# Turning x by transposes, the first conditioning loads from ScalarE's queue, and more of the conditioning sums on VectorE, in a hybrid convolution and attention layer

## The chip, the cores and the metric

The kernel runs on one core of a Trainium2 chip. The metric is device time in microseconds (us) for one launch. A core has TensorE (PE, matrix products into PSUM; PEld is its weight load), VectorE (DVE), ScalarE (ACT), GpSimd (POOL) and SyncE (SP). SP issues the DMA loads in the kernel before; in the profile SPq is the issuing side of SP.

## The reference

One decoder layer on x of 512 tokens by 2048 features, float32, with a conditioning vector c of 2048. What matters here is its beginning:

```python
mod = silu(c) @ w_ada + b_ada                 # 2048 -> 3 * 2048
shift, scale, gate = split(mod, 3)
h = rms_norm(x, g_pre) * (1 + scale) + shift  # rstd per token, scale and shift per feature
p = h @ w_in                                  # split into nine parts
u = cv * sigmoid(cg)                          # the first two parts of p: 2 * 1024 columns
```

Behind that come a causal depthwise convolution with a layer norm, differential attention over 8 heads, gates, two branch projections, a merge, an output projection, a norm and the residual. The change does not touch them.

## The kernel before

Products of float32 operands are written as sums of float32r parts: `split` makes a high part on ScalarE (`wh_`, `hh`) and a low part on VectorE (`wl_`, `hl`), and `mm3` (L163 is its matmul) issues three matmuls for each pair of operands. Features lie on the partitions, in 16 tiles of 128 features by 512 tokens: `xn[k]` is x times rstd, `h[k]` the normalised and conditioned input.

The opening ("start" in the code) does four things.

- *x.* SP loads x as 16 tiles, `xs[t][j]`, of 128 tokens by 512 features. `squares(t)` sums squares of a token tile, two quarters on ScalarE and two on VectorE. `scales(t0)` turns the sums of two token tiles into rstd on VectorE and puts it on a diagonal, `diag[t]`. `norm_x(j, ts)` multiplies blocks of x with that diagonal on TensorE (L236), which turns and scales them at once, into a PSUM bank `pxt`; ScalarE copies each 128x128 block into `xn` (L239).
- *Conditioning.* `ada(c0, width, npe)` makes shift and scale for `width` features. `ada_load` fetches 16 parts of `w_ada` for each (tiles `ada`, 512 KB each, seven buffers, tag `ar`). `npe` of the 16 parts go through TensorE (L273, bank `pa`): four calls with 32 columns of weights each, in four column strips of the array. The other parts are summed on VectorE (L276, L278, `acc`). In the end small products (L288, or L293 and L294, bank `pm`) bring the sums onto the partitions, VectorE adds the biases (L298 to L300), and ScalarE and VectorE make `hf` and its two parts. `GROUPS` lists the groups: first column, width, `npe`.
- *The first two parts of p.* `conv_gemm(k0, nk)` multiplies the finished features with all 2048 columns of cv and cg (bank `pc`). The first group copies its banks into `part` on ScalarE; each later group is added to `part` on VectorE (L339).
- *Order.* Up to the first group, the program order on TensorE, ScalarE and VectorE is written by hand (`manual_schedule`). Behind it `interleave` gives the order in which the convolution's steps, the next conditioning group's and what is left of x (`rest`) are emitted, and a planner arranges the engines' queues. DMA issues keep to their queue's order.

PSUM banks `g` (four) serve both `pxt` and `pc`; banks `m` (four) serve `pm`, `pa` and small things.

Of the kernel before, what the change touches and what calls it, by code (L numbers as in the profile page):

```python
# [9 lines left out]
F32 = mybir.dt.float32  # L10
# [34 lines left out]
ST = (3, 6, 6, 6, 13, 10)  # L45
# columns of shift and scale, and how many of the 16 parts of the sum TensorE takes
GROUPS = ((0, 128, 16), (128, 128, 16), (256, 256, 16), (512, 256, 16), (768, 256, 16),
          (1024, 512, 12), (1536, 512, 0))


@with_exitstack
def hybrid_trunk(ctx: ExitStack, tc: tile.TileContext, x, c, w_ada, b_ada, g_pre, g_post, w_in,
# [18 lines left out]

# [1 line left out]
    ident = cpool.tile([P, P], F32, name="ident")  # L73
# [47 lines left out]
    def rsqrt1(z, name):  # L121
        """1 / sqrt(z) for one value per partition."""
        y, t, zh = [small(1, f"{name}_{n}") for n in "yth"]
        yi, zi = y.bitcast(I32), z.bitcast(I32)
        nc.vector.tensor_single_scalar(yi, zi, 1, op=ALU.logical_shift_right)
        nc.vector.tensor_scalar(yi, yi, -1.0, 1597463007.0, op0=ALU.mult, op1=ALU.add)
        nc.vector.tensor_scalar_mul(zh, z, -0.5)
        for _ in range(3):
            nc.vector.scalar_tensor_tensor(t, y, zh, y, op0=ALU.mult, op1=ALU.mult)
            nc.vector.scalar_tensor_tensor(y, t, 1.5, y, op0=ALU.add, op1=ALU.mult)  # L130
        return y

    def paced(instruction):
        """Keep the instructions so marked in program order on their engine."""
        if PACE:
            tc.stamp_issue_order_token(instruction.ins, "paced")
        return instruction
# [35 lines left out]
    def interleave(*gens):  # L173
        """Advance generators, each given with its number of steps, in proportion."""
        gens = [[g, n, 0] for g, n in gens]
        while gens:
            g = min(gens, key=lambda e: (e[2] + 1) / e[1])
            g[2] += 1
            if next(g[0], StopIteration) is StopIteration:
                gens.remove(g)  # L180

    # ================= start: conditioning, normalised input, conv gates =================
    with tc.tile_pool(name="ps0", bufs=1, space=PSUM) as ps0, tc.tile_pool(name="ap", bufs=1) as ap:
        def gbank(name):
            return ps0.tile([P, S], F32, tag="g", bufs=4, name=name)
# [18 lines left out]
        nc.vector.memset(halves[64:, 1:2], 1.0)  # L204
        # x * rstd, features on the partitions
        xn = [page(f"xn_{kt}") for kt in range(KT)]
        ss = small(KT, "xss")

        diag = [None] * NT

        def squares(t):
            for j in range(4):
# [5 lines left out]
                else:  # L218
                    nc.scalar.activation(sq, xs[t][j], AF.Square, accum_out=ss[:, i:i + 1])

        def scales(t0):
            """diag(rstd) of 2 * 128 tokens."""
            z = small(2, f"xz_{t0}")
            nc.vector.reduce_sum(z, ss[:, 4 * t0:4 * t0 + 8].rearrange("p (t j) -> p t j", j=4),
                                 axis=mybir.AxisListType.X)
            nc.vector.tensor_scalar(z, z, 1.0 / D, EPS, op0=ALU.mult, op1=ALU.add)
            r = rsqrt(z, 2, f"xr_{t0}")
            for t in (t0, t0 + 1):
                diag[t] = ap.tile([P, P], F32, name=f"diag_{t}")
                nc.vector.tensor_scalar_mul(diag[t], ident, r[:, t - t0:t - t0 + 1])  # L230

        def norm_x(j, ts):
            for t in ts:
                pt = gbank(f"pxt_{t}_{j}")
                for i in range(4):
                    nc.tensor.matmul(pt[:, i * P:(i + 1) * P], xs[t][j][:, i * P:(i + 1) * P], diag[t],  # L236
                                     start=True, stop=True)
                for i in range(4):
                    nc.scalar.copy(xn[4 * j + i][:, t * P:(t + 1) * P], pt[:, i * P:(i + 1) * P])  # L239
                yield  # L240
# [7 lines left out]

        def ada_load(k0, nk, c0, width):
            raws = []  # L250
            for a in range(2):
                raw = ap.tile([P, nk, width], F32, tag="ar", bufs=AR, name=f"ada_{a}_{c0}_{k0}")
                nc.sync.dma_start(out=raw, in_=ada_v[:, k0:k0 + nk, a * D + c0:a * D + c0 + width])
                raws.append(raw)
            return raws

        def ada(c0, width, npe):
            """shift and scale of columns c0..c0+width, and h for these features; npe of the 16 parts of the
            sum on TensorE, the others on VectorE."""
            nk, nb, kb = 1024 // width, width // P, c0 // P  # L260
# [4 lines left out]
            for k0 in range(0, KT, nk):  # L265
                raws = ada_load(k0, nk, c0, width)
                for kk in range(k0, k0 + nk):
# [81 lines left out]
        with tc.manual_schedule(engines={mybir.EngineType.PE, mybir.EngineType.Activation, mybir.EngineType.DVE}):  # L349
            squares(0)  # L350
            squares(1)
            scales(0)
            squares(2)
            interleave((norm_x(0, (0, 1)), 1))
            squares(3)
            scales(2)
            interleave((norm_x(1, (0, 1)), 1))
            group = ada(*GROUPS[0])
            for _ in range(2):
                next(group)  # L360
            interleave((norm_x(0, (2, 3)), 1))
            next(group)
            early[0, 0, 0] = conv_wsplit(0, 1, 0, 4, 0, C_CV)
            interleave((group, 1))
        for g, a, c0 in ((0, 1, C_CG), (1, 0, C_CV)):
            early[0, g, a] = conv_wsplit(0, 1, g, 4, a, c0)
        rest = [norm_x(j, ts) for j, ts in ((1, (2, 3)), (2, range(4)), (3, range(4)))]
        rest = (None for g in rest for _ in g)
        for i, (c0, width, _) in enumerate(GROUPS[:-1]):
# [25 lines left out]

    # ================= main part =================
    ps1 = ctx.enter_context(tc.tile_pool(name="ps1", bufs=1, space=PSUM))
# [16 lines left out]
    def gemm2(src, c0, rhs, nk, name):  # L414
        """Two output tiles [128 features, tokens] of columns c0..c0+256."""
        ps = [bank("g", 4, f"pg_{name}_{f}") for f in range(2)]
# [10 lines left out]

    # lambda
    lt = small(HD, "lt")
# [10 lines left out]

# [1 line left out]
    cvo = [None] * 8  # L442
# [40 lines left out]

# [1 line left out]
    vt = [None] * 2  # L485
# [72 lines left out]
    for pair in range(4):  # L558
# [13 lines left out]
        for f in range(2):  # L572
            head(pair * 2 + f, qs[f], ks[f])
# [1 line left out]
    # h = [[B11, B12], [B21, B22]], halves of the features by halves of the tokens:  # L575
    # T1 = B11 - B12, T2 = B22 + T1, T3 = B12 - B22, T4 = B21 - T2
    H2 = S // 2
# [55 lines left out]

    # ================= gates =================
    front.close()
# [13 lines left out]
    def gemm_blocks(src, c0, name):  # L649
        """Two output tiles [128 features, tokens] of h @ src[:, c0:c0+256], by 7 products of 2x2 blocks.  # L650

        a11 a12 / a21 a22: features by halves of the sum.  Returns (c11 in PSUM, [.. c12], [c21 c22])."""
        r1 = wraw(src, 0, KH, c0, 256, f"{name}_1")
# [7 lines left out]
        def prod(ps, w, b, first):  # L661
            """Add a product to what the bank holds (read between the products)."""
            hi, lo = w
            for k in range(KH):
                mm3(ps[:, :H2], (hi[:, k, :], lo[:, k, :]), b[k], first and k == 0, k == KH - 1, not first, ordered)
            pump(rate[0])
# [31 lines left out]
    def silu2(i, z, ta, tb):  # L698
        """2 * silu of the two output tiles."""
        g0, g1 = temp(f"g0_{i}"), temp(f"g1_{i}")  # L700
# [7 lines left out]

    # channel layer norm and swish of the convolution, its gate
    hg = small(8, "hg")  # L710
# [84 lines left out]

    # ================= branch projections, gated merge =================
    # 2 * (sigmoid(m_conv) * y_conv + sigmoid(m_attn) * y_attn)
    def gemm_y(src, c0, rhs, name):
# [42 lines left out]
    def gate(n):  # L841
        """Columns n * 512.. of (c @ w_ada's gate part + b_ada) * g_post, on all partitions."""
        bg = temp(f"bg_{n}")
# [45 lines left out]

    # ================= output projection, tokens on the partitions =================  # L890
    fss = small(16, "fss")
# [15 lines left out]
    for n in range(4):  # L907
# [19 lines left out]
        if n < 3:  # L927
            for t in range(NT):
                out_evac(n, t, ps[t])
    # what the first three parts give to the mean square  # L930
    nc.vector.reduce_sum(zp, fss.rearrange("p (t n) -> p t n", n=4)[:, :, :3], axis=mybir.AxisListType.X)
# [46 lines left out]
```

## Time and profile before

| what | value |
|---|---|
| time, median of 3 runs | 1445.52 us (1444.5 to 1447.1) |
| span of the profiled execution | 1448.4 us |
| TensorE busy | 1413.6 us, 98% |
| VectorE busy | 1053.0 us, 73% |
| ScalarE busy | 534.2 us, 37% |
| first convolution matmul (`pc`) starts | 33.05 us |
| first matmul of the attention's values (`pv`) starts | about 258 us |

The profile is of one execution; its span lies 2.9 us above the median of the runs, and the page shows no time of the execution outside its span. Busy time counts instructions at work; a busy TensorE is not TensorE at its peak, since matmuls are pipelined. The granted clock (PEclk) is given as a share of 2.4 GHz; 0.50 is 1.2 GHz.

### The profile page before, as it was taken

To read this page: it belongs to the slowest core of one execution; us is meant where nothing else is said; L and a number is where in the kernel's file an instruction comes from. 1 tells how busy PE (TensorE), PEld (TensorE's weight loads), DVE (VectorE), ACT (ScalarE), POOL (GpSimd) and SP (SyncE) were. 2 spreads that over 40 slices of the span, in tenths; PEclk is the share of its full clock that TensorE was granted. 3 is DMA by queue.
4 is the path that set the end of the run, shared out by engine and by line. 5 is a ranking of instruction groups with operands and counts; after the bars stand their busy time and mean duration, and the time that the engine had idled before them with its cause. 6 is when DMAs were issued, how large, how long until landed. Compare 5 with 4: busy or idle time off the path is not lost.

```text
span 1448.4 us, 20732 instructions
## 1 busy us (share of the span) xinstructions
PE 1413.6 (98%) x8191; PEld 1200.4 (83%) x8191; DVE 1053.0 (73%) x1720; ACT 534.2 (37%) x901; POOL 1.8 (0%) x8
## 2 busy tenths in 40 slices
PE   4999999999999999999999999999999999999997
PEld 4776778787777877688999999999998888888885
DVE  4466785988888888588997888877767448656645
ACT  4622233223444244434544444444445323222230
POOL 0000000000000000000000000000000000000000
PEclk9999999999999999999999999999999999999999
DMA  9878653232223323124654555533369647267543
GB/s 285 264 255 291 215 167 130 88 131 87 66 81 102 102 67 109 66 95 135 209 165 160 187 178 191 188 121 132 126 226 349 224 137 233 95 207 243 189 145 145
DMA packets 178466, 238.62 MB, mean 165 GB/s; under 512 B 7793, under 2 KB 118722, under 8 KB 177474
## 3 DMA queue, kind: packets, MB, share of 16 engines
q1 hardware_dynamic: 178370, 237.31, 49.5%
q8 instruction: 64, 1.05, 0.3%
q14 instruction: 32, 0.26, 0.1%
HBM read 210.02 MB, written 27.26 MB: 164 GB/s over the span
## 4 chain that ended last, share of the span: by engine, by line
PE 93%; DVE 3%; DMA 1%; ACT 1%; issue 1%; SPq 0%; DVEq 0%; ACTq 0%
PE pc L163 12%; PE pw L163 12%; PE py_ya L163 6%; PE py_yc L163 6%; PE pv L163 6%; PE pg_k L163 6%; PE pg_q L163 5%; PE pg_az L163 5%; PE x_ma L163 5%; PE x_mc L163 5%; PE y_mc L163 3%; PE z_mc L163 3%; PE z_ma L163 3%; PE y_ma L163 3%; PE x_cz L163 2%; PE y_cz L163 2%
## 5 line engine op out<-in xcount | busy, mean ns | idle before, releaser
L468 DVE SCALAR_TENSOR_TENSOR cacc<-u,cw,cacc 128x511 f32<-128x511 f32 (+14 forms) x240 | 164.4, 729 | 0.0
L163 PE MATMUL pc<-hh,wh_c 128*128 128x512 f32 x256 | 102.9, 408 | 1.1 <-ACT hh L141 1.1
L163 PE MATMUL pc<-hh,wl_c 128*128 128x512 f32 x256 | 101.0, 398 | 1.5 <-DVE wl_c L142 1.4
L163 PE MATMUL pc<-hl,wh_c 128*128 128x512 f32 x256 | 101.7, 397 | 0.0
L339 DVE TENSOR_TENSOR part<-pc,part 128x512 f32<-128x512 f32 x96 | 66.0, 691 | 46.9 <-PE pc L163 45.8
L163 PE MATMUL pw<-wh_o,mh 128*128 128x512 f32 x224 | 89.0, 397 | 0.0
L163 PE MATMUL pw<-wh_o,ml 128*128 128x512 f32 x224 | 87.3, 390 | 0.0
L163 PE MATMUL pw<-wl_o,mh 128*128 128x512 f32 x224 | 87.2, 389 | 0.0
L141 ACT CAST wh_c<-wr_c 128x1024 fp32r<-128x1024 f32 (+1 forms) x36 | 34.6, 960 | 112.5 <-PE pc L163 85.6
L141 ACT CAST wh_o<-wr_o 128x1024 fp32r<-128x1024 f32 x28 | 29.5, 1053 | 104.5 <-PE pw L163 93.0
L163 PEld LDWEIGHTS pc<-hh,wh_c 128*128 128x128 f32 x256 | 49.0, 192 | 17.9 <-issue 3.3
L856 DVE SCALAR_TENSOR_TENSOR accg<-adag,cact,accg 128x512 f32<-128x512 f32 x60 | 45.0, 750 | 24.0 <-DMA adag<-in_w_ada_dram 22.8
L163 PEld LDWEIGHTS pc<-hh,wl_c 128*128 128x128 f32 x256 | 49.1, 192 | 15.7 <-issue 2.5
L142 DVE TENSOR_TENSOR wl_o<-wr_o,wh_o 128x1024 fp32r<-128x1024 f32 x28 | 34.2, 1221 | 34.0 <-ACT wh_o L141 34.0
L163 PEld LDWEIGHTS pc<-hl,wh_c 128*128 128x128 f32 x256 | 49.3, 192 | 10.2 <-issue 0.4
L163 PE MATMUL pv<-wh_v,hh 128*128 128x512 f32 x128 | 51.2, 400 | 0.9 <-DVE part L339 0.9
L142 DVE TENSOR_TENSOR wl_c<-wr_c,wh_c 128x1024 fp32r<-128x1024 f32 (+1 forms) x36 | 39.7, 1104 | 16.5 <-ACT wh_c L141 16.4
L163 PE MATMUL pg_q<-hh,wh_q 128*128 128x512 f32 x128 | 51.1, 399 | 0.0
L163 PE MATMUL pg_k<-hh,wl_k 128*128 128x512 f32 x128 | 51.1, 399 | 0.0
L163 PE MATMUL pg_q<-hl,wh_q 128*128 128x512 f32 x128 | 50.9, 397 | 0.0
L163 PE MATMUL pg_az<-hl,wh_az 128*128 128x512 f32 x128 | 50.7, 396 | 0.0
L163 PE MATMUL pv<-wl_v,hh 128*128 128x512 f32 x128 | 50.6, 395 | 0.0
(358 smaller groups left out, 4312.7 us busy)
## 6 DMA issues: line engine op xcount, KB each, us to landing
ada<-in_w_ada_dram SPq DMA_DIRECT2D x64, 512.0 KB, 6.1
wr_ma<-in_w_in_dram SPq DMA_DIRECT2D x16, 1024.0 KB, 5.5
wr_mc<-in_w_in_dram SPq DMA_DIRECT2D x16, 1024.0 KB, 5.0
adag<-in_w_ada_dram SPq DMA_DIRECT2D x32, 512.0 KB, 4.2
wr_o<-in_w_o_dram SPq DMA_DIRECT2D x16, 1024.0 KB, 5.1
wr_c<-in_w_in_dram SPq DMA_DIRECT2D x28, 512.0 KB, 5.0
wr_v<-in_w_in_dram SPq DMA_DIRECT2D x8, 1024.0 KB, 5.2
wr_q<-in_w_in_dram SPq DMA_DIRECT2D x8, 1024.0 KB, 5.3
```

Of the source, the lines that this page charges most:

```text
L141: nc.scalar.copy(hi, src)
L142: i = nc.vector.tensor_tensor(lo, src, hi.bitcast(F32), op=ALU.subtract)
L163: mm = nc.tensor.matmul(ps, a[p], b[q], start=start and i == 0, stop=stop and i == 2, skip_group_check=more)
L339: nc.vector.tensor_tensor(part[i], ps[f], part[i], op=ALU.add)
L468: paced(nc.vector.scalar_tensor_tensor(cvo[t][:, s:], u[t][:, :S - s], wj, cvo[t][:, s:], op0=ALU.mult, op1=ALU.add))
L856: nc.vector.scalar_tensor_tensor(acc, raw[:, k, :], s1, acc, op0=ALU.mult, op1=ALU.add)
```

## The change

`GROUPS` gives fewer parts to TensorE in four of the seven groups. x is turned with transposes that don't need rstd, into one bank per feature tile with all four token tiles; rstd is spread over the partitions by a product of ones and the diagonal (bank `prs`), copied to `rsb` by ScalarE, and VectorE multiplies each `pxt` bank with it into `xn`. Of the 16 feature tiles eight are turned inside the hand-written order and eight behind it. The four loads of the first conditioning group are issued on ScalarE's queue, ahead of the hand-written part.

```diff
-GROUPS = ((0, 128, 16), (128, 128, 16), (256, 256, 16), (512, 256, 16), (768, 256, 16),
-          (1024, 512, 12), (1536, 512, 0))
+GROUPS = ((0, 128, 16), (128, 128, 16), (256, 256, 12), (512, 256, 10), (768, 256, 10),
+          (1024, 512, 8), (1536, 512, 0))
...
+        rsb = ap.tile([P, S], F32, name="rsb")
+        prs = mbank("prs0")
         def scales(t0):
...
             for t in (t0, t0 + 1):
-                diag[t] = ap.tile([P, P], F32, name=f"diag_{t}")
-                nc.vector.tensor_scalar_mul(diag[t], ident, r[:, t - t0:t - t0 + 1])
-        def norm_x(j, ts):
-            for t in ts:
-                pt = gbank(f"pxt_{t}_{j}")
-                for i in range(4):
-                    nc.tensor.matmul(pt[:, i * P:(i + 1) * P], xs[t][j][:, i * P:(i + 1) * P], diag[t],
-                                     start=True, stop=True)
-                for i in range(4):
-                    nc.scalar.copy(xn[4 * j + i][:, t * P:(t + 1) * P], pt[:, i * P:(i + 1) * P])
+                diag = ap.tile([P, P], F32, tag="diag", bufs=2, name=f"diag_{t}")
+                nc.vector.tensor_scalar_mul(diag, ident, r[:, t - t0:t - t0 + 1])
+                nc.tensor.matmul(prs[:, t * P:(t + 1) * P], ones, diag, start=True, stop=True)
+            ts = slice(t0 * P, (t0 + 2) * P)
+            nc.scalar.copy(rsb[:, ts], prs[:, ts])
+        pxt = [None] * KT
+        def turn(ks, ts):
+            for k in ks:
+                if pxt[k] is None:
+                    pxt[k] = gbank(f"pxt_{k}")
+                for t in ts:
+                    nc.tensor.transpose(pxt[k][:, t * P:(t + 1) * P],
+                                        xs[t][k // 4][:, k % 4 * P:(k % 4 + 1) * P], ident)
+        def norm_x(ks):
+            for k in ks:
+                nc.vector.tensor_tensor(xn[k], pxt[k], rsb, op=ALU.mult)
+        def turn_norm(ks):
+            for k in ks:
+                turn((k,), range(NT))
+                norm_x((k,))
                 yield
...
-        def ada_load(k0, nk, c0, width):
+        def ada_load(k0, nk, c0, width, queue=nc.sync):
...
-                nc.sync.dma_start(out=raw, in_=ada_v[:, k0:k0 + nk, a * D + c0:a * D + c0 + width])
+                queue.dma_start(out=raw, in_=ada_v[:, k0:k0 + nk, a * D + c0:a * D + c0 + width])
...
+        begun = {(0, k0): ada_load(k0, 8, 0, 128, nc.scalar) for k0 in (0, 8)}
...
-                raws = ada_load(k0, nk, c0, width)
+                raws = begun.pop((c0, k0), None) or ada_load(k0, nk, c0, width)
...
         with tc.manual_schedule(engines={mybir.EngineType.PE, mybir.EngineType.Activation, mybir.EngineType.DVE}):
-            squares(0)
-            squares(1)
-            scales(0)
-            squares(2)
-            interleave((norm_x(0, (0, 1)), 1))
-            squares(3)
-            scales(2)
-            interleave((norm_x(1, (0, 1)), 1))
+            for t in range(NT):
+                squares(t)
+                turn(range(4), (t,))
+                if t % 2:
+                    scales(t - 1)
+            norm_x(range(4))
             group = ada(*GROUPS[0])
+            next(group)
+            turn(range(4, 8), range(NT))
+            norm_x(range(4, 8))
             for _ in range(2):
                 next(group)
-            interleave((norm_x(0, (2, 3)), 1))
-            next(group)
             early[0, 0, 0] = conv_wsplit(0, 1, 0, 4, 0, C_CV)
             interleave((group, 1))
...
-        rest = [norm_x(j, ts) for j, ts in ((1, (2, 3)), (2, range(4)), (3, range(4)))]
-        rest = (None for g in rest for _ in g)
+        rest = turn_norm(range(8, KT))
```

## Rows read from the trace of the kernel before

**Rows 1.** The page's busy times, with shares of the span and instructions

```profile
PE 1413.6 (98%) x8191; PEld 1200.4 (83%) x8191; DVE 1053.0 (73%) x1720; ACT 534.2 (37%) x901; POOL 1.8 (0%) x8
```

**Rows 2.** Windows by stage: stretch, length, busy PE, PEld, DVE, ACT, POOL, clock, DMA

```profile
33.05:56.20 23.15, 23.15 (x162) 20.14 (x162) 6.21 (x16) 18.73 (x60) 0.00 (x0) 0.93 0.78 249
56.20:72.20 16.00, 16.00 (x118) 11.00 (x117) 12.84 (x23) 4.48 (x11) 0.00 (x0) 1.00 0.88 294
72.20:99.90 27.70, 27.65 (x167) 20.05 (x166) 19.75 (x30) 8.87 (x12) 0.00 (x0) 1.00 0.83 279
...
126.80:153.80 27.00, 27.00 (x139) 15.90 (x138) 15.78 (x23) 3.00 (x3) 0.00 (x0) 0.98 0.93 321
153.80:207.50 53.70, 52.16 (x225) 42.42 (x225) 46.39 (x68) 14.89 (x17) 0.00 (x0) 0.95 0.59 190
```

**Rows 3.** The chain that ended last, to 34 us: start, duration, what

```profile
13.92 3.25 SPq L253
...
17.21 8.02 DMA ada<-in_w_ada_dram
...
33.05 1.07 PE pc L163 x2
```

**Rows 4.** DMA of the first 60 us, in 40 slices of 1.5 us

```profile
GB/s 0 87 238 317 149 173 388 396 393 389 362 307 290 291 291 318 371 311 290 292 296 271 348 279 320 370 362 368 352 349 369 139 22 210 175 35 58 295 40 264
```

**Rows 5.** Timeline of SP's issues: start, duration, what, count

```profile
12.55 6.38 SPq L253 DMA_DIRECT2D ada<-in_w_ada_dram  x4
```

**Rows 6.** Timelines of VectorE and TensorE ahead of the first convolution matmul

```profile
17.58 0.68 DVE L216 CUSTOM_DVE_ANT_0 xsq<-x 128x512 f32<-128x512 f32 x1
...
21.53 0.16 DVE L224 TENSOR_REDUCE xz<-xss 128x2 f32<-128x8 f32 x1 [3.26 <-ACT xsq L219]
...
24.10 0.48 DVE L230 TENSOR_SCALAR diag<-ident,xr_y 128x128 f32<-128x128 f32 x2
...
29.73 0.34 PE L288 MATMUL pm<-halves,accp 128*128 128x2 f32 x2
```

**Rows 7.** Bursts on TensorE, from the chain that ended last, to 250 us

```profile
51.82 4.46 PE pxt L236 x40
...
64.23 1.86 PE pa L273 x32
...
69.04 0.34 PE pm L288 x4
...
136.91 0.97 PE pa L273 x2
...
205.94 1.68 PE pm L294 x16
```

**Rows 8.** TensorE by line and form, to 260 us: busy, mean ns, idle before

```profile
L273 PE MATMUL pa<-ada,c 128*32 128x256 f32 x192 | 12.8, 384 | 0.0
L273 PE MATMUL pa<-ada,c 128*32 128x512 f32 x48 | 9.1, 601 | 0.0
```

**Rows 9.** Timeline of TensorE in the attention stage, around a burst of transposes

```profile
611.92 0.60 PE L533 MATMUL pt<-ident,t 128*128 128x128 f32 x4
612.27 0.48 PE L163 MATMUL pg_az<-hh,wl_az 128*128 128x512 f32 x1
```

**Rows 10.** VectorE by line and form, to 260 us

```profile
L339 DVE TENSOR_TENSOR part<-pc,part 128x512 f32<-128x512 f32 x96 | 66.0, 691 | 46.9 <-PE pc L163 45.8
...
L278 DVE SCALAR_TENSOR_TENSOR acc<-ada,cact,acc 128x512 f32<-128x512 f32 x36 | 25.3, 747 | 0.0
...
L284 DVE COPY accp<-pa 128x256 f32<-128x256 f32 x3 | 1.3, 419 | 0.0
```

**Rows 11.** Windows of TensorE: stretch, length, busy time, granted clock, DMA

```profile
149.77:153.76 3.99, 3.99 (x33) 0.87 1.06 386
153.76:159.56 5.80, 5.80 (x15) 0.50 0.40 138
205.78:207.48 1.70, 1.70 (x17) 1.00 0.96 326
```

More of the change, by code (lines that the diff above doesn't have):

```diff
@@ L207, in hybrid_trunk @@
         ss = small(KT, "xss")
-        diag = [None] * NT
         def squares(t):
```

## The prediction

> **What bounds the kernel now.** I read the busy shares first: TensorE is busy for 98% of the span, so what counts is work taken from it, work added to it, and time in which it is made to wait [rows 1]. Then the stages of the opening in one table of windows [rows 2]. Before 33.05 us, when the first convolution matmul starts [rows 3], TensorE still waits; from there it is busy for all but 0.05 us of the stages shown up to 153.8 us, while VectorE has room in each: 16.9 us of 23.2, 3.2 of 16.0, 8.0 of 27.7 and 11.2 of 27.0. Only in 153.8 to 207.5 us is VectorE nearly full (46.4 of 53.7), and there TensorE is idle for 1.5 us. The reader should keep two budgets apart: the instant at which the convolution starts, and TensorE's work after it. The profiled span is 1448.4 us, 2.9 us above the median of the three runs, 1445.5; the page gives no time outside the span, so I work out differences and take them off the median. A change of 0.2%, 2.9 us, is about what a measurement of this kernel can tell from none.
>
> **Turning x.** Before, a 128x128 product with a diagonal is two matmul records, and 40 of these records took 4.46 us, 111 ns each [rows 7], so 223 ns a block. Of the 64 blocks, 24 are done ahead of 33.05 us and 40 after it: 8.9 us. After the change 32 of the 64 are turned ahead of the convolution and 32 behind. A true transpose is one record in the attention stage, and a burst of four held TensorE for 0.35 us, from 611.92 to 612.27 us [rows 9]: 88 ns each, 2.8 us for 32. Saved: 6.1 us (at 56 ns each, half of a product's record, 7.1; with 0.09 us more a burst for the change of kind that I cannot see in the row, 5.4). The Trainium skill, "TensorE: Matmul & The Clock Gate", Terms, calls its transpose mode four times faster for FP32; the row gives 2.5 times, and by the rule 7.1 us would be saved. I go by the row.
>
> **The multiplication by rstd** moves from 64 ScalarE copies to 16 VectorE products of 128x512 out of PSUM, priced like the part additions, 0.69 us [rows 10]. Eight of them lie in 33 to 56 us, where VectorE has 16.9 us free, so 5.5 us cost nothing there; without that cover they would be 5.5 us. The other eight lie on the chain into the first matmul (below).
>
> **Conditioning sums.** TensorE loses 4, 6 and 6 of 16 parts in the three groups of 256 columns and 4 of the remaining 12 in that of 512. Today they are 192 records with 12.8 us and 48 records with 9.1 us busy [rows 8]. Four calls run side by side: 32 records of 256 columns took 1.86 us, 58 ns each, but two records of 512 columns alone still held TensorE for 0.97 us [rows 7]. So half-filled rounds cost as much as full ones, and dropping parts saves less than in proportion. For 256 columns 128 records remain: 7.4 us if packed, 12 if each step is a burst by itself; I take 9.9, 2.9 us saved. For 512 columns 32 records remain, one part in each of eight steps: 3.7 us packed, 7.8 as eight rounds of 0.97; I take 7.1, 2.0 us saved. Together 4.9 us (2.1 to 10.8).
>
> **The final sums get dearer.** A group done wholly on TensorE closes with one small product for each block: four records, 0.34 us. As soon as VectorE holds a share, each block needs four products, as in the last group: sixteen records for 16 columns' worth, 1.68 us [rows 7]. A 256-column group then needs sixteen too, so three groups cost 3 x 1.34 = 4.0 us more (5.0 at the 125 ns a record that the 512-column group shows in its 3.99 us for 32 [rows 11]).
>
> TensorE's work after its start: -6.1 - 4.9 + 4.0 = -7.0 us (-2.5 to -13.9).
>
> **VectorE's new work.** 32 multiply-adds of 128x256 at some 0.42 us (the copy of that shape; the 512 form is 0.75) are 13.4 us, and 8 of 128x512 are 6.0 [rows 10]. By stage: 3.4 us into 3.2 spare, 5.0 into 8.0, 5.0 into the stage that follows, for which I assume the same room, 6.0 into 11.2. It is late in the first alone, but a part addition that stands behind a sum keeps one of four PSUM banks from the next convolution matmul. I charge 1.3 us (0 if the planner always puts sums into the gaps; 9 if nearly half of the 19 us falls on TensorE).
>
> **The instant at which the convolution starts.** Today the last square ends at 18.3 us, but the scales wait until 21.53 because ScalarE copies turned blocks before its own last squares [rows 6]; the conditioning landed only at 25.23 [rows 3]. After the change both go. If x lands as now: scales and diagonals 3.05 us (21.53 to 24.58) after 18.4, giving 21.5; two small products and a 256-column copy, 1.1; eight products on VectorE in a row, 5.5, giving 28.1; behind them in VectorE's program order the copy of the conditioning sum, 0.3; then small product to first matmul as today, 29.73 to 33.05, less one weight cast that can go earlier, 2.7: 31.1 us, 2.0 earlier. So a new serial stretch eats most of the removed waits.
>
> But x will not land as now. The conditioning's 2.1 MB start beside x's 4.2 MB on the same DMA engines, which moved 290 to 396 GB/s from 9 to 24 us and less in the slices from 3 to 9 us (877 against some 1560 over four slices of 1.5 us: about 1.0 MB of room) [rows 4]. The 2.1 MB took 7 us at 290 GB/s; less what fits into the room, x is 0 to 4.5 us later. I take 3: start at 34.1 us, 1.0 later than now (bounds -2.0 and, with ScalarE held up, +4.3, below). Issuing from ScalarE frees 6.38 us of SP's issuing [rows 5], and SP's weight loads follow x sooner; they were not what the first matmul waited for.
>
> **Sum:** -7.0 + 1.3 + 1.0 = -4.7 us, 1440.8 us.
>
> **Rivals.**
> *The opening is late (0.20).* On SP the third conditioning load held the queue for 3.25 us, and the four took 6.38 us where an issue without a hold-up takes about 0.4; as I read it, they stood behind packets still waiting [rows 3, 5]. On ScalarE the same hold-up stands in front of its tanh and of eight squares, and VectorE's squares and scales, some 11 us in a row, stand behind that tanh. If the fourth issue ends near 14 us instead of 3, the convolution starts at 35.5 to 37.4 us, up to 4.3 later than now, and the time is -7.0 + 1.3 + 4.3: 1444.1 us. Against it: alone on the engines, the first half of these 2.1 MB would be gone within 4 us [rows 4]. The Trainium skill says in "Trainium Kernel Development and Optimization", Key Constraints, that issuing from several engines only saves issue time, since all queues share 16 DMA engines and interleave; by that rule x is always late and this rival or its milder form holds. The trace has one data queue, so no row here shows two interleaving.
>
> *VectorE becomes the bound (0.14), the one on the other side.* The place is the three stages from 56 to 127 us: a sum ahead of a part addition holds a PSUM bank. For it: the 153.8 to 207.5 us stage, where sums fill VectorE and TensorE idles 1.5 us and its matmuls spread. Against: from 72 us the spare time is above what is added. Without stalls the change is -6.0 us, so with 6 us on TensorE it is a wash and from 8.9 us, nearly half of the 19, it is slower by over 0.2%. At 9 us: 1448.5 us.
>
> *The clock falls in the new final sums (0.06).* After 3.99 us of single-column products the granted clock was 0.50, 1.2 GHz, from 153.76 to 159.56 us: 5.80 us for the work of 2.9 [rows 11]. Three new such stretches would cost 8.7 us: 1449.5. Against: these are 1.7 us each, and the stretch of that length at 205.78 us was at full clock. One dip leaves 1443.7, so it decides from the third.
>
> *More gain (0.10).* Sums near their packed price (-8 instead of -4.9) and x landing as now: -6.1 - 8 + 4.0 - 2.0 = -12.1 without stalls, 1433.4 us.
>
> **How the numbers follow.** The forecast itself has 0.50, with a range of its own from 1437 to 1444. Shares of faster by over 0.2%, within 0.2%, and slower: forecast 0.42, 0.08, 0; late opening 0.04, 0.09, 0.07 (with stalls too); VectorE 0.01, 0.05, 0.08; clock 0, 0.01, 0.05; more gain 0.10, 0, 0. Sums 0.57, 0.23, 0.20. The range for 8 in 10 runs from 1434 to 1449: it leaves out the most of "more gain" and the far half of VectorE and clock.
>
> **What the profile after would show.** Half as many records for turning x, in bursts of four near 0.35 us; about 64 fewer conditioning records of 256 columns but bursts that stay near 1 us; sixteen small records at three group ends, 1.7 us each; the first convolution matmul between 31 and 36 us, behind eight VectorE products; VectorE over 0.9 busy from 56 to 72 us with TensorE idle below 1 us; TensorE's stretch from first convolution matmul to 258 us today shorter by 4 to 8 us. Wrong would be: ScalarE's squares starting after 14 us, TensorE idle on a part addition or an accumulator, or a granted clock of 0.5 after a new final sum.

## The result, and the profile after

The change makes the kernel slower: 1455.81 us (median of four runs, 1454.79 to 1457.22) against 1445.78 (four runs, 1444.5 to 1447.1); the ratio is 1.0062 [1.0043, 1.0082], some 6 to 12 us. The forecast was 1440.8, with a range from 1434 to 1449.

| point in the profiled execution, us | before | after |
|---|---|---|
| VectorE's last square of x ends | 18.26 | 24.84 |
| first convolution matmul starts | 33.05 | 41.19 |
| first matmul of the attention's values starts | 258.29 | 263.06 |
| span | 1448.4 | 1453.0 |

From the attention's first matmul on, the traces of both take 1190 us, and so does the trace of every kernel below: what the traces differ by is decided in the opening. The page's busy times of after answer to [rows 1]; TensorE has 5.5 us less to do, and the kernel is longer all the same:

```profile
span 1453.0 us, 20544 instructions
...
PE 1408.1 (97%) x8091; PEld 1194.9 (82%) x8091; DVE 1077.4 (74%) x1776; ACT 523.0 (36%) x839; POOL 1.8 (0%) x8
```

The timeline of after, up to the first convolution matmul (start, duration, what; in brackets the idle time before it and what ended it):

```profile
0.73 9.05 ACTq L268 DMA_DIRECT2D ada<-in_w_ada_dram  x4
...
6.57 11.60 SPq L95 DMA_DIRECT2D x<-in_x_dram  x12
9.81 1.28 ACT L195 ACT_TABLE_LOAD   x1 [9.81 <-DMA x<-in_x_dram]
...
24.15 0.69 DVE L214 CUSTOM_DVE_ANT_0 xsq<-x 128x512 f32<-128x512 f32 x1 [0.64 <-DMA x<-in_x_dram]
...
25.66 0.16 DVE L225 TENSOR_REDUCE xz<-xss 128x2 f32<-128x8 f32 x1 [0.81 <-ACT xsq L217]
...
32.19 0.23 DVE L447 TENSOR_TENSOR lt<-lamv 128x64 f32<-128x64 f32 x1 [3.16 <-DMA lamv<-in_lam_k_dram]
...
32.59 4.29 DVE L249 TENSOR_TENSOR xn<-pxt,rsb 128x512 f32<-128x512 f32 x7
...
41.19 1.20 PE L163 MATMUL pc<-hh,wh_c 128*128 128x512 f32 x4 [1.02 <-ACT hh L141]
```

Three things are to be seen. ScalarE issues until 9.8 us, and its table load waits for that. The last squares wait for x's DMA: the one that began at 17.58 before [rows 6] begins at 24.15. And VectorE, done with the scales, stands idle for 3.16 us ahead of a product `lt` that belongs to the attention's lambda and has nothing to do with x: the planner put it ahead of the eight products with rstd, and its operand had not landed.

What each queue moved between 1 and 11 us (packets, MB, share of 16 engines), in after:

```profile
q10 hardware_dynamic: 2691, 1.36, 48.1%
q1 hardware_dynamic: 715, 1.16, 42.5%
```

and in before, where SP's queue is alone:

```profile
q1 hardware_dynamic: 1309, 2.23, 75.0%
```

q10 is ScalarE's queue with the conditioning, q1 is SP's with x. Together they moved 0.3 MB more than SP's queue alone, so almost everything that the conditioning got, x lost: 1.07 MB by 11 us. By 15 us even the 0.3 MB are gone, since from 9 to 15 us before moved 392 GB/s and after 332. From 1 to 15 us after shows

```profile
q10 hardware_dynamic: 4154, 2.10, 55.3%
q1 hardware_dynamic: 1025, 1.71, 42.1%
```

and before

```profile
q1 hardware_dynamic: 2168, 3.80, 83.5%
```

The two queues moved 3.81 MB, the one 3.80: x had lost the conditioning's whole 2.1 MB.

The bursts of x's transposes behind the start, from the chain that ended last in after:

```profile
45.21 0.59 PE pxt L244 x4
...
48.57 0.87 PE pxt L244 x8
...
52.47 0.87 PE pxt L244 x8
...
56.62 1.46 PE pxt L244 x12
```

They answer to these `pxt` bursts of before and to the one of 4.46 us in [rows 7]:

```profile
38.68 1.09 PE pxt L236 x8
...
42.52 0.89 PE pxt L236 x8
...
43.53 1.00 PE pxt L236 x8
...
47.30 1.78 PE pxt L236 x16
```

3.79 us for 32 transposes, against 9.22 for the 80 records of before: 5.4 us saved. TensorE's conditioning records and small products in after, by line and form (answers to [rows 8]), up to 263 us:

```profile
L290 PE MATMUL pa<-ada,c 128*32 128x256 f32 x128 | 11.6, 386 | 0.0
L311 PE MATMUL pm<-ones,acc 128*128 128x1 f32 x56 | 9.1, 248 | 0.0
L290 PE MATMUL pa<-ada,c 128*32 128x512 f32 x32 | 8.7, 603 | 0.0
L310 PE MATMUL pm<-halves,accp 128*128 128x1 f32 x40 | 6.9, 241 | 0.0
```

A third of the records went, and 1.2 us of 12.8 and 0.4 of 9.1 with them. The chain shows why: a burst is priced by rounds, of which a part costs as much as the whole. 10 records of 256 columns took as long as 12, and a pair of 512 columns nearly 1 us by itself:

```profile
62.01 0.99 PE pa L290 x12
...
72.06 0.98 PE pa L290 x10
...
143.96 0.98 PE pa L290 x2
```

In before 16 records of 256 columns took no longer than these 10:

```profile
56.29 1.00 PE pa L273 x16
```

The two waits of TensorE between 154 and 207 us that cost more than 1 us, in after:

```profile
182.84 0.50 PE L163 MATMUL pc<-hh,wl_c 128*128 128x512 f32 x1 [2.75 <-DVE wl_c L142]
195.78 0.50 PE L163 MATMUL pc<-hh,wl_c 128*128 128x512 f32 x1 [1.73 <-DVE wl_c L142]
```

Before has one, of 1.43 us (at 191.05). On VectorE four sums stand ahead of the first of these weight parts, in program order:

```profile
178.92 2.73 DVE L295 SCALAR_TENSOR_TENSOR acc<-ada,cact,acc 128x512 f32<-128x512 f32 x4
181.56 1.22 DVE L142 TENSOR_TENSOR wl_c<-wr_c,wh_c 128x1024 fp32r<-128x1024 f32 x1
```

The two traces differ by 4.6 us and the timed runs by 10.0. A span lies 1.7 to 2.2 us below the time of the same execution in every one for which both are known (after: 1453.0 and 1454.79 us). So the traced execution of before, with its span of 1448.4, stands for some 1450 us, 4 to 5 above its median, and that of after is 1.0 below its own, which makes up the other 5.4 us. The granted clock tells why in part. Between its start and 258 us the profiled execution of before was at 0.50 for 10.2 us, 6.8 of them in the stretch that [rows 11] shows and 3.41 here (stretch, length, busy TensorE, clock, DMA):

```profile
33.26:36.67 3.41, 3.41 (x9) 0.50 0.97 315
```

Up to 263 us after has only 160.50 to 163.91, behind the group of 1024:

```profile
156.70:160.10 3.40, 3.40 (x34) 1.00 0.90 307
160.50:163.91 3.41, 3.41 (x10) 0.50 0.00 0
```

So before spent 6.8 us more than after at half the clock, which is 3.4 us of work. Such stretches vary between executions (the mean granted clock of before's timed runs goes from 0.993 to 0.998), so differences of 1 to 3 us between two traces are not read as effects below; the ratios of timed runs decide.

### The profile page after: what moved, and what is told of

Same layout as the page of the kernel before. It is cut to its first block, busy times and chain, and to the rows that moved or that the text cites. A ratio compares the mean times of both kernels' runs of the same rounds, so it can differ in the third digit from the quotient of the medians.

```text
span 1453.0 us, 20544 instructions
## 1 busy us (share of the span) xinstructions
PE 1408.1 (97%) x8091; PEld 1194.9 (82%) x8091; DVE 1077.4 (74%) x1776; ACT 523.0 (36%) x839; POOL 1.8 (0%) x8
## 4 chain that ended last, share of the span: by engine, by line
PE 93%; DVE 3%; DMA 2%; ACT 1%; issue 1%; SPq 0%; DVEq 0%; ACTq 0%
PE pc L163 12%; PE pw L163 12%; PE pg_k L163 6%; PE py_ya L163 6%; PE py_yc L163 6%; PE pv L163 6%; PE pg_az L163 5%; PE pg_q L163 5%; PE x_ma L163 5%; PE x_mc L163 5%; PE y_mc L163 3%; PE z_mc L163 3%; PE z_ma L163 3%; PE y_ma L163 3%; PE x_cz L163 2%; PE y_cz L163 2%
## 5 line engine op out<-in xcount | busy, mean ns | idle before, releaser
L163 PE MATMUL pg_q<-hh,wl_q 128*128 128x512 f32 x128 | 50.5, 395 | 0.0
```

The source lines that it names most:

```text
L163: mm = nc.tensor.matmul(ps, a[p], b[q], start=start and i == 0, stop=stop and i == 2, skip_group_check=more)
```

## The experiments

The change has three parts: the loads on ScalarE's queue (L), the new `GROUPS` (G) and the turning (T). Five runs undo or isolate one part or two, and with before and after they make a table of all combinations but one (G with L). Before was timed again beside each set of runs, with medians from 1447.02 to 1448.14 us, so ratios are compared here and not times.

| kernel | parts | ratio to before | first convolution matmul, us |
|---|---|---|---|
| before | none | 1 | 33.05 |
| e3 | L | 1.0049 [1.0037, 1.0062] | 38.08 |
| e6 | G | 1.0024 [1.0015, 1.0034] | 32.22 |
| e5 | T | 0.9995 [0.9985, 1.0005] | 32.60 |
| e1 | T, G | 1.0032 [1.0021, 1.0044] | 31.40 |
| e2 | T, L | 1.0020 [1.0011, 1.0029] | 40.66 |
| after | T, G, L | 1.0062 [1.0043, 1.0082] | 41.19 |

**e1, the conditioning loads back on SP.** The theory: the late start is due to the loads beside x. The rival: VectorE's serial stretch makes it.

```diff
-        begun = {(0, k0): ada_load(k0, 8, 0, 128, nc.scalar) for k0 in (0, 8)}
+        begun = {}
```

> The changed kernel, with the first four conditioning loads back on SP's queue behind x. Theory A (the loads on ScalarE's queue are what costs: they share the DMA engines with x and hold ScalarE until 9.8 us): the last square on VectorE is back from 24.2 to near 17.6 us, the first convolution matmul comes at 33 to 36 us instead of 41.2, and the time falls from 1455.8 to 1448 to 1451 us. Theory B (the conditioning sums on VectorE cost it, not the opening): the first matmul may move, but the time stays above 1453 us. Theory C (the eight products with rstd in a row are the late part): the first matmul stays at 39 us or later.

Measured: 1452.5 us, ratio 1.0032. The start is at 31.40 us and the last square ends at 17.58: the loads cause the late start, 9.8 us of it. But the time fell by only 0.3%, some 4 us, to a value between those expected by its theories A and B. One reason is a new wait, of TensorE on the weights' fourth tile. Its row in TensorE's timeline of e1:

```profile
41.48 0.50 PE L163 MATMUL pc<-hh,wh_c 128*128 128x512 f32 x1 [3.37 <-DVE xn L249]
```

VectorE's next product into `xn`, which frees a PSUM bank for TensorE, stood in program order behind a weight part whose cast had waited for its DMA. The rest shows only in the clock: the profiled execution, 1448.9 us at a mean granted clock of 0.996, was the fastest of six; the other five took 1452.2 to 1452.8 at 0.992 or 0.993. In which stretch they lost it, no trace here shows.

**e2, the old groups.** The theory: the new sums cost time. The rival: they save, and the opening alone costs.

```diff
-GROUPS = ((0, 128, 16), (128, 128, 16), (256, 256, 12), (512, 256, 10), (768, 256, 10),
-          (1024, 512, 8), (1536, 512, 0))
+GROUPS = ((0, 128, 16), (128, 128, 16), (256, 256, 16), (512, 256, 16), (768, 256, 16),
+          (1024, 512, 12), (1536, 512, 0))
```

> The changed kernel with the conditioning sums divided between the engines as before the change. Theory A: the sums are nearly even, 4 to 5 us less on TensorE against 4 us more in the final small products, so the time stays within 3 us of 1455.8. Theory B: the time falls by 6 us or more, to under 1450 us.

Measured: 1450.5 us, ratio 1.0020. With the start as late as after's, 217.2 us instead of 221.9 lie between it and the attention's first matmul. The new groups cost 4.7 us there; the waits behind `wl_c` shrink to the one of 1.43 us that before has. So the theory holds, and the late opening costs the rest.

**e3, before with the loads on ScalarE alone.**

```diff
-        def ada_load(k0, nk, c0, width):
+        def ada_load(k0, nk, c0, width, queue=nc.sync):
...
-                nc.sync.dma_start(out=raw, in_=ada_v[:, k0:k0 + nk, a * D + c0:a * D + c0 + width])
+                queue.dma_start(out=raw, in_=ada_v[:, k0:k0 + nk, a * D + c0:a * D + c0 + width])
...
+        begun = {(0, k0): ada_load(k0, 8, 0, 128, nc.scalar) for k0 in (0, 8)}
...
-                raws = ada_load(k0, nk, c0, width)
+                raws = begun.pop((c0, k0), None) or ada_load(k0, nk, c0, width)
```

> The kernel before with one edit: the first four conditioning loads issued from ScalarE's queue. Theory A: ScalarE is held for some 9 us and x lands some 6 us later, so the first convolution matmul comes 3 to 7 us after the 33.05 us of before and the time rises by 3 to 7 us, to 1449 to 1453 us. Theories B and C: within 2 us of 1445.8, since the conditioning lands earlier than the 25.2 us that the first matmul waited for.

Measured: 1454.9 us, ratio 1.0049, the dearest single part. The last square ends at 24.33 us and the convolution starts 5.0 us late. Lambda's wait is here too, though nothing of VectorE's work was edited: SP issues lambda's first load at 27.95 us here, at 49.98 in before, and the planner put its product into the opening.

**e4, lambda's products behind the opening.** After, with the products of `lt` held behind the last `u`.

```diff
+        last_u = [None]
...
-                        nc.vector.scalar_tensor_tensor(u[i], th, 1.0, part[i], op0=ALU.add, op1=ALU.mult)
+                        last_u[0] = nc.vector.scalar_tensor_tensor(u[i], th, 1.0, part[i], op0=ALU.add, op1=ALU.mult)
...
-    for i in range(2):
-        nc.vector.tensor_tensor(lt, lamv[:, 2 * i, :], lamv[:, 2 * i + 1, :], op=ALU.mult)
-        nc.vector.reduce_sum(le[:, i:i + 1], lt, axis=mybir.AxisListType.X)
+    with tc.issue_after(last_u[0].ins):
+        for i in range(2):
+            nc.vector.tensor_tensor(lt, lamv[:, 2 * i, :], lamv[:, 2 * i + 1, :], op=ALU.mult)
+            nc.vector.reduce_sum(le[:, i:i + 1], lt, axis=mybir.AxisListType.X)
```

> The changed kernel with VectorE's lambda products put behind its last instruction of the convolution input, where the changed kernel has the first of them between the diagonals and the eight products with rstd, waiting 3.2 us for a load of lambda's rows. Theory A with this wait as a part of the loss: the first convolution matmul comes 1.5 to 2.5 us earlier than 41.2 and the time falls by as much, to 1453 to 1454.5 us. Rival: the eight products wait for ScalarE's copy of rstd and for turned banks anyway, and the time stays within 0.7 us of 1455.8.

Measured: 1454.1 us, ratio 1.0044 [1.0031, 1.0056]; its interval and after's overlap. In its timeline the eight products begin at 30.55 us, right behind `rsb`:

```profile
30.55 4.92 DVE L249 TENSOR_TENSOR xn<-pxt,rsb 128x512 f32<-128x512 f32 x8 [1.33 <-ACT rsb L234]
```

The convolution starts at 38.11 us, so lambda's place cost 3.1 of the 9.8 us between e1 and after, and the loads the other 6.7. Of the 3.1, 2.0 are the later begin of the eight products. The other 1.0 goes with the 16 transposes among them, which took 2.35 us in e4, 3.68 in after, and 3.67 in e8 below at a granted clock of 0.50. Of the 3.1, 2.2 came back at 47.05 us as a wait of TensorE behind the fourth weight tile, cast at 45.05, as in e1: a start that is earlier than its weights gains little.

**e5, the turning alone.** After with both edits of e1 and e2.

```diff
+GROUPS = ((0, 128, 16), (128, 128, 16), (256, 256, 16), (512, 256, 16), (768, 256, 16),
+          (1024, 512, 12), (1536, 512, 0))
...
+        begun = {}
```

> The changed kernel with both the loads on SP's queue and the old division of the sums: of the change, only x turned by transposes and multiplied by rstd on VectorE is left. If the two other parts are what costs, each by itself: the first convolution matmul at 31 to 33 us, TensorE's stretch from there to the attention's values 217 to 220 us (217.2 with the old sums, 225 to 226 with the new ones), and a time 4 to 8 us under the kernel before beside it. If the transposes' serial stretch on VectorE costs: no faster than the kernel before.

Measured: 1447.06 us against 1448.14, ratio 0.9995: no difference. 32 transposes behind the start are cheap here too, but the timelines of ScalarE and TensorE in e5 have these rows:

```profile
40.52 0.62 ACT L141 CAST wh_c<-wr_c 128x512 fp32r<-128x512 f32 x1 [4.17 <-DMA wr_c<-in_w_in_dram]
...
42.52 0.50 PE L163 MATMUL pc<-hh,wh_c 128*128 128x512 f32 x1 [3.25 <-DVE xn L249]
```

Before has no such wait up to 60 us: the cast of that tile runs at 38.19 us there, and bursts of turning x stand between the first steps. 3.25 us, of the 5.4 that the transposes save, are handed to the weights. Not all of it is TensorE being earlier: the tile is later too. SP's queue has seven conditioning loads between the third weight tile and the fourth where that of before has five, so the fourth goes out later. In e5

```profile
33.56 1.27 SPq L151 DMA_DIRECT2D wr_c<-in_w_in_dram  x2
```

and in before

```profile
32.02 0.34 SPq L151 DMA_DIRECT2D wr_c<-in_w_in_dram  x1
```

**e6, the new groups alone**, in before.

```diff
+GROUPS = ((0, 128, 16), (128, 128, 16), (256, 256, 12), (512, 256, 10), (768, 256, 10),
+          (1024, 512, 8), (1536, 512, 0))
```

> The kernel before with only the new division of the sums. Theory B as now seen (final small products +4 us, 1 to 3 us saved on the sums, VectorE in the way for 3 to 6 us): the stretch from the first convolution matmul to the attention's values grows from 225 to 229 to 233 us and the time by 4 to 8 us. Rival, as predicted: within 2 us of the kernel before.

Measured: 1451.7 us, ratio 1.0024, 3.5 us and a little less than the 4 to 8 expected: the sums cost without any other part. The waits in TensorE's timeline of e6 are after's:

```profile
178.23 0.50 PE L163 MATMUL pc<-hh,wl_c 128*128 128x512 f32 x1 [2.75 <-DVE wl_c L142]
191.18 0.50 PE L163 MATMUL pc<-hh,wl_c 128*128 128x512 f32 x1 [1.73 <-DVE wl_c L142]
```

From the table the part G costs 0.24% (before to e6), 0.37% (e5 to e1) and 0.42% (e2 to after). The part L costs 0.49% (before to e3), 0.25% (e5 to e2) and 0.30% (e1 to after). The part T makes no clear difference without L (-0.05% from before to e5, +0.08% from e6 to e1), but saves 0.29% with it (e3 to e2): there the convolution starts at 38 us or later, and no wait for the fourth weight tile follows in either trace.

**e7 and e8, sharing or ScalarE held?** After's loads sit on a second queue and also hold ScalarE's instructions for 9 us. e7 leaves two of the four loads there, e8 issues all four from GpSimd.

```diff
-        begun = {(0, k0): ada_load(k0, 8, 0, 128, nc.scalar) for k0 in (0, 8)}
+        begun = {(0, 0): ada_load(0, 8, 0, 128, nc.scalar)}
```

> The changed kernel with only the first two of the four loads on ScalarE's queue, which SP's issues of before let through without a hold-up. If ScalarE held up is the larger part: ScalarE's tanh runs by 5 us, VectorE starts its squares as before, and the first convolution matmul comes at 34 to 36 us, 5 or more earlier than 41.2. If sharing the DMA engines with x is: half the bytes, so x is some 3 us late instead of 6.5, and the first matmul comes at 37 to 39 us.

```diff
-        begun = {(0, k0): ada_load(k0, 8, 0, 128, nc.scalar) for k0 in (0, 8)}
+        begun = {(0, k0): ada_load(k0, 8, 0, 128, nc.gpsimd) for k0 in (0, 8)}
```

> The changed kernel with the four first loads issued from GpSimd's queue instead of ScalarE's: they still start beside x, but ScalarE is not held. If sharing the DMA engines is the cause: the last square still ends at 22 to 25 us and the first convolution matmul comes at 37 us or later. If the hold-up of ScalarE is: the first convolution matmul comes at 32 to 35 us. A slow start of the loads from GpSimd would show as a conditioning sum that comes after the eight products.

Measured: e7 1454.7 us, ratio 1.0048 [1.0033, 1.0063], last square 22.62, start 36.32 us, between the two ranges expected. e8 1455.85 us, ratio 1.0057 [1.0042, 1.0071]. The timeline of e8:

```profile
0.74 1.28 ACT L195 ACT_TABLE_LOAD   x1 [0.74 <-PEq L979]
1.73 1.01 POOL L268 DMA_DIRECT2D ada<-in_w_ada_dram  x1
...
3.31 2.65 POOL L268 DMA_DIRECT2D ada<-in_w_ada_dram  x3
...
25.75 0.16 DVE L225 TENSOR_REDUCE xz<-xss 128x2 f32<-128x8 f32 x1 [1.53 <-ACT xsq L217]
...
41.27 0.96 PE L163 MATMUL pc<-hh,wh_c 128*128 128x512 f32 x3 [1.02 <-ACT hh L141]
```

ScalarE is free from the beginning, its squares wait for x instead, and the convolution starts at 41.27 us, where after's starts at 41.19. Both stand behind lambda's wait (2.61 us in e8), which could hide a difference ahead of it; but the second scales, ahead of that wait, begin at 25.75 us against 25.66 in after. That ScalarE was held cost nothing; the bytes beside x made it late. Half of the bytes (e7) leave x's last square 4.4 us late instead of 6.6. The convolution of e7 starts 4.9 us earlier than after's, more than these 2.2, since lambda's first product stands behind the eight products there and waits 1.31 us; in the ratios the intervals of e7 and after overlap.

**e9, the opposite of G.** Before with all 16 parts of the group of 1024 on TensorE.

```diff
-          (1024, 512, 12), (1536, 512, 0))
+          (1024, 512, 16), (1536, 512, 0))
```

> The kernel before with one number changed the other way: in the group at column 1024 TensorE takes all 16 parts instead of 12. If half-filled rounds and dearer final products are why giving parts to VectorE does not pay: the sums of 512 columns stay at 8 to 9 us for a third more parts, the final products of that group fall from 4.0 to 0.7 us, VectorE loses 6 us of work, the drop of the clock behind the products is gone, and the time falls by 4 to 8 us. Rival, by work in proportion: 2 us more on the sums against 3.3 us less, within 2 us of the kernel before.

Measured: 1439.53 us against 1447.02, ratio 0.9943 [0.9931, 0.9955]. By line and form, up to 262 us:

```profile
L273 PE MATMUL pa<-ada,c 128*32 128x512 f32 x64 | 8.0, 598 | 0.0
...
L288 PE MATMUL pm<-halves,accp 128*128 128x2 f32 x24 | 3.0, 230 | 0.0
L294 PE MATMUL pm<-ones,acc 128*128 128x1 f32 x16 | 1.8, 245 | 0.0
```

64 records take less than the 48 of before (9.1 us [rows 8]), as every round is filled. The group closes with 8 small products in 0.79 us where [rows 11] shows 33 records in 3.99, the wait of 1.43 us behind `wl_c` is gone, and behind the products TensorE's clock stays up, as the window of the next 20 us shows (columns as above):

```profile
145.95:165.95 20.00, 20.00 (x89) 1.00 0.89 298
```

As an estimate from the two traces, 1.1 us on the records, 3.2 on the closing, 1.4 of wait and 3.4 of clock (6.8 us at half in before) add to some 9 us, where the ratio gives 8.2. The fall of the clock goes with that closing: the traces of all twelve kernels with 32 small products there show 0.50 for 3.4 or 6.8 us, beginning in the closing or within 1.5 us behind it, and those of e9 and e11, with 8, show none. For this group the move that the change makes has the wrong sign; for the groups of 256 columns e9 says nothing.

**e10, only tiles 8 to 15 turned**, with the opening of before up to the start.

```diff
+        rsb = page("rsb")
+
+        def turn_norm(ks):
+            prs = mbank("prs0")
+            for t in range(NT):
+                nc.tensor.matmul(prs[:, t * P:(t + 1) * P], ones, diag[t], start=True, stop=True)
+            nc.scalar.copy(rsb, prs)
+            for k in ks:
...
+                    nc.tensor.transpose(pt[:, t * P:(t + 1) * P],
+                                        xs[t][k // 4][:, k % 4 * P:(k % 4 + 1) * P], ident)
+                nc.vector.tensor_tensor(xn[k], pt, rsb, op=ALU.mult)
+                yield
...
-        rest = [norm_x(j, ts) for j, ts in ((1, (2, 3)), (2, range(4)), (3, range(4)))]
+        rest = [norm_x(1, (2, 3)), turn_norm(range(8, KT))]
```

> The kernel before with its own opening, where only the eight feature tiles behind the hand-written part are turned by transposes and multiplied by rstd on VectorE. If the transposes' saving of some 5.5 us is real and was only eaten by an earlier wait for the fourth weight tile: the first convolution matmul stays at 33 us, that wait is 1 us or less, and the time falls by 3 to 5 us. If the wait comes back in full: within 1.5 us of the kernel before.

Measured: 1444.09 us, ratio 0.9974 [0.9963, 0.9985]. The start is at 33.64 us, and no wait on weights follows up to 60 us. The first tiles are still turned by products there, and SP issues the fourth weight tile behind five conditioning loads, as in before, at 32.61 us; the run doesn't part the two. Here the transposes show their gain.

**e11, e9 and e10 together.**

```diff
-          (1024, 512, 12), (1536, 512, 0))
+          (1024, 512, 16), (1536, 512, 0))
...
+        rest = [norm_x(1, (2, 3)), turn_norm(range(8, KT))]
```

> The two edits together (the eight later tiles turned, all 16 parts on TensorE in the group at column 1024). If they act in different stages the gains add, 7 to 12 us under the kernel before; if both only fill a wait that is set elsewhere, no more than the larger of the two alone.

Measured: 1436.74 us against 1447.02, ratio 0.9922 [0.9909, 0.9934]: faster than both kernels, and nearly the sum of the two (0.83%).

**e12, e5 with the fourth weight tile loaded ahead** of the 256-column conditioning loads on SP.

```diff
+        held = [None]
...
-                queue.dma_start(out=raw, in_=ada_v[:, k0:k0 + nk, a * D + c0:a * D + c0 + width])
+                with tc.issue_after(held[0].ins) if held[0] else nullcontext():
+                    queue.dma_start(out=raw, in_=ada_v[:, k0:k0 + nk, a * D + c0:a * D + c0 + width])
...
+                fourth = wp.tile([P, 1, 4 * P], F32, tag="wr", name="wr_c_0_1_1")
+                held[0] = nc.sync.dma_start(out=fourth, in_=w_in[0].rearrange("(t p) n -> p t n", p=P)[
+                    :, 0:1, C_CG + 4 * P:C_CG + 8 * P])
+                early_raw[0, 1, 1] = fourth
```

> The turned x alone (loads on SP, old sums), with the convolution's fourth weight tile issued ahead of the 256-column conditioning loads instead of behind three of them. If the 3.2 us that TensorE stood at 42.5 us in the run without this edit was a wait for that tile (it landed at 40.4 us): it lands at 35 to 37.5 us, the wait is under 1 us, and the time is 2 to 3 us below that run, some 3 us under the kernel before. If the wait is VectorE's or ScalarE's own order: it stays above 2 us and the time stays that of the kernel before.

Measured: 1446.34 us against 1447.46, ratio 0.9991 [0.9982, 1.0]; e5 had 0.9995. The wait became shorter, not absent (TensorE's timeline of e12):

```profile
40.75 0.50 PE L163 MATMUL pc<-hh,wh_c 128*128 128x512 f32 x1 [2.09 <-DVE xn L249]
```

SP had moved the lambda loads ahead of the tile, which was issued at 34.93 us only. So this run doesn't show what the whole turning gives with the tile in time; e10 shows it for half the tiles, and e3 to e2 with a late start.

## Why the prediction was wrong, point by point

Its sum, term by term, with what the traces of before and after show (us):

| term | predicted | measured |
|---|---|---|
| turning x behind the start | -6.1 | -5.4 (9.22 to 3.79) |
| conditioning sums off TensorE | -4.9 | -1.6 (12.8 + 9.1 to 11.6 + 8.7) |
| final small products | +4.0 | +4.0 (three stretches like 70.38 to 72.06 us, for 0.34 each) |
| waits for VectorE | +1.3 | +3.0 (2.75 + 1.73 less 1.43) |
| the instant at which the convolution starts | +1.0 | +8.1 (33.05 to 41.19) |
| sum | -4.7 | +8.1 |

+8.1 lies inside the +6 to +12 of the timed runs. The execution of before that was profiled lost 3.4 us more to the clock than that of after; less these, it is 4.7, and the spans differ by 4.6. Of the 12.8 us by which the sum is off, 7.1 are the start, 3.3 the conditioning sums, 1.7 the waits and 0.7 the turning.

**The instant at which the convolution starts failed, by 7.1 us.** The case "if x lands as now" was right: 31.1 us forecast, 31.40 in e1. The step that failed is "x is 0 to 4.5 us later. I take 3", and in it the room of about 1.0 MB that the conditioning was to fill in the slices from 3 to 9 us. By 11 us the two queues had moved only 0.3 MB more than one, and by 15 us no more at all: x was behind by the conditioning's whole 2.1 MB. Its last square came 6.6 us later, which is 2.1 MB at some 320 GB/s. A gap in the throughput row was taken for room. With e4, 6.7 us of start, against e1, are due to this sharing. The other 3.1 are lambda's place, which the prediction did not have: SP's loads were followed past the weights only, not to the loads that moved up, and the planner placed their consumer ahead of the products. The rival "the opening is late" had the right place and the wrong cause. Its hold-up is there (ScalarE's issuing ends at 9.8 us), but e8 shows that it costs nothing. The rule cited with it, of the Trainium skill, "Trainium Kernel Development and Optimization", Key Constraints, that issuing from several engines saves only issue time because all share the 16 engines, agrees with these runs: with another issuer x was as late (second scales at 25.75 against 25.66 us, convolution at 41.27 against 41.19). None of the three signs of being wrong that the prediction names stands behind the loss; the start at 41.19 us, where it expected 31 to 36, does.

**The conditioning sums were mis-sized, by 3.3 us.** "Half-filled rounds cost as much as full ones" was right, but the values taken, between packed and rounds, lay too far from rounds: the 1.6 us saved are less than the lowest bound given (2.1), and the 32 records of 512 columns took 8.7 us, more than the 7.8 of eight rounds. With the final small products, rightly sized at +4.0, the move costs where it was forecast to save 0.9: 128 records for 192 save 1.2 us and the closings cost 4.0. e6 and e2 show that the move as a whole costs, and e9 that the opposite gains for one group.

**Waits for VectorE** were forecast in the stages from 56 to 127 us, and none came there: TensorE is busy for all of 56 to 127 us in after. They came from 154 to 207 us, the stage that the prediction itself had called nearly full (46.4 of 53.7 us [rows 2]), by program order: four sums ahead of a weight part, though the group whose sums run there is unchanged. Why the planner's order differs there stays open. The rival "VectorE becomes the bound" was right that sums would make TensorE wait, wrong in the stage and in what stood behind them, and small: 3.0 us.

**Turning x** was right: 5.4 saved, the lower of the bounds given. The figure of the Trainium skill, "TensorE: Matmul & The Clock Gate", Terms, four times faster for FP32, is not met: 12 transposes in 1.46 us and 8 in 0.87 are 122 and 109 ns each, about twice as fast as a product's 223 ns. Whether this call turns on the mode that the figure is for, no row names. What the prediction did not see is that the saved time is waited for where the fourth weight tile sets the pace, and that the tile itself is issued later (e5), so that this part alone gives nothing measurable.

**The clock** did not fall behind the new stretches of 1.7 us in any of the six traces with the new groups; its rival was rightly small.

## What to carry to other kernels

Before a load is moved to a second queue, count its bytes as taken from whatever the first queue is moving, and ask which of the two is needed first; dips in the throughput row were not room here. Price small matmuls by rounds and by their closing work: taking a third of the records out of rounds that still ran saved 1.6 us of 21.9, and filling the rounds was the gain (e9). A start that is made earlier, or work that is taken out ahead of a transfer, is worth only what the next arrival leaves of it (e1, e4, e5).

## What the hardware showed unexpectedly

- Two queues had nearly equal shares of the bytes: 1.36 MB against 1.16 from 1 to 11 us, though one has 2691 packets and the other 715. From 9 to 15 us the two together moved 332 GB/s, where x alone had moved 392.
- Four loads issued from ScalarE's stream held it for 9.05 us and two of them for 1.08 (e7); from GpSimd's they took 1.01 and 2.65 us, with the convolution's start unchanged.
- 512-column conditioning records in column strips: 64 take 8.0 us, 48 take 9.1, 32 take 8.7.
- The granted clock fell to 0.50 behind 3.40 us of single-column products (after, 1.00 during them) and stayed at 1.00 behind the three stretches of some 1.7 us and behind the 0.79 us of e9.
